# Splitting the weight slabs of the recurrent mixers one block ahead, and keeping their two parts in DRAM

## The chip, the cores and the metric

The kernel runs on one core of a Trainium2 chip. The metric is the device time of one execution in microseconds. The kernel before took 2590.76 us, the median of 3 runs (2590.26 to 2594.12). All engine times below come from one profiled execution of it.

## What is computed

Everything is fp32, on 512 tokens of width 1024. Block 1 has two layers, each with a latent attention, a dilated attention, gates, and an output projection that is added to x. Block 2 has two layers too: a mixer, then a convolutional feed-forward part. The mixer of its first layer is the recurrent one: an HGRN2 part and an RWKV7 part, side by side. Cut to what matters here:

```python
# block 1, each of 2 layers
h = rms_norm(x, norm_g[layer]); p = h @ w_in[layer]
...
x = x + jnp.concatenate([a, b], axis=-1) @ w_out[layer]
# block 2, first layer: the recurrent mixers
h = _rmsnorm(x, norm_g[l, 0]) * (1.0 + scale) + shift
p = h @ ab_w_in[j]
pa, pb = p[..., :A_IN], p[..., A_IN:]
q, f_fwd, f_bwd, i, g = jnp.split(pa, 5, axis=-1)
y_a = _hgrn2_mixer(q, f_fwd, f_bwd, i, g, lower_bounds[l], hgrn_norm_g[j])
y_b = _rwkv7_mixer(pb, rwkv_mu[j], ...)
mix = jnp.concatenate([y_a, y_b], axis=-1) @ ab_w_out[j]
x = x + gate * mix
...
x = x + gate * _conv_ffn(h, ffn_w_up[l], ffn_conv_w[l], ffn_conv_b[l], ffn_w_down[l])
```

## The kernel before

Activations lie transposed, features on the 128 partitions and the 512 tokens along the row. A product with fp32 precision is made of three TensorE passes over split operands: an operand a is held as a high part (a rounded to fp32r by ScalarE, `ACT`) and a low part (a minus the high part, by VectorE, `DVE`), and `mm3` adds high x high, high x low and low x high. A weight matrix is cut into slabs of 128 partitions x 1024 elements (512 KB): eight tiles of 128 x 128, one for each 128 rows of the contraction.

`wslab` (L70) brings one slab in: a DMA issued by the sync engine (`SP`) into a buffer `wraw`, a copy on ACT into `whi` (L75), a subtraction on DVE into `wlo` (L76). Each of the three tags has three buffers that are taken in turn, whoever asks. `gemm` (L91) takes such a slab and issues 24 matmuls of 128x512 into one PSUM tile. The three slabs that follow a norm are split early by `prepare` (L119) and multiplied by `early`.

The stages, in order:
- Block 1, twice (`block1_mixers`, L416): six gemms for the latent attention, four gates (`gate`, L426), the latent attention, V products of the dilated attention (weights `w_dv`, with the ada slabs of block 2 streamed beside them by `adaln`), then four head pairs with six gemms each (`operands`, L578) between the steps of `attention` (L604), four more gates, and `out_proj` (L191) with eight gemms on `w_out`. While it runs, x comes back from DRAM in one transfer of 2 MB (`load_x`, L1618), `add_x` (L229) adds each product to it, and it is written to DRAM again piece by piece (`to_dram`, L1608).
- The recurrent mixers (`m2`, L1680): `rwkv_lora` takes the three prepared slabs; `rwkv_g` takes three slabs for each of four head pairs P; `rwkv_p`, `rwkv_a`, `rwkv_t`, `rwkv_c1`, `rwkv_c2`, `rwkv_c3` are the recurrence, a long chain of small matmuls and vector steps. Between its steps `hgrn_fill` (L1237) computes the HGRN projections (4 slabs `w_hi`, 16 slabs `w_hg`) and writes them to DRAM (`spill`). Then the HGRN units run beside the first half of the output projection (`out_proj_steps`, eight half slabs of 128x512), and the second half (eight half slabs) follows.
- The feed-forward part, the second mixer (`m3`) and its feed-forward part.

The program is written as one stream; a scheduler places each engine's instructions in a fixed order, and each engine, and each DMA queue, works through its own in that order. SP issues nearly all DMAs, so a DMA whose buffer isn't free holds back those behind it. The buffers are taken in the order of the code:

```python
        self.w = es.enter_context(tc.tile_pool(name="w", bufs=3))
...
        hi, lo = out or [self.w.tile(shape, F32R, name=t, tag=t) for t in ("whi", "wlo")]
        nc.scalar.activation(hi, raw, AF.Copy)
        (eng or nc.vector).tensor_tensor(lo, raw, hi.bitcast(F32), op=ALU.subtract)
```

Of the kernel before, what the change touches and what calls it, by code (L numbers as in the profile page):

```python
# [24 lines left out]
class Ctx:  # L25
# [44 lines left out]
    def wslab(self, src, shape, raw=None, eng=None, out=None):  # L70
        nc = self.nc
        if raw is None:
            raw = self.wraw(src, shape)
        hi, lo = out or [self.w.tile(shape, F32R, name=t, tag=t) for t in ("whi", "wlo")]
        nc.scalar.activation(hi, raw, AF.Copy)  # L75
        (eng or nc.vector).tensor_tensor(lo, raw, hi.bitcast(F32), op=ALU.subtract)  # L76
        return hi, lo
# [41 lines left out]
    def prepare(self, src, raw=None, eng=None):  # L119
        pool, tag = ((self.px, "px"), (self.py, "py"), (self.pg, "pg"))[len(self.ready)]  # L120
        self.ready.append((self.wslab(src, [128, KD, 128], raw, eng), pool.tile([128, S], F32, name="pe", tag=tag)))

    def split(self, hi, lo, src):
# [67 lines left out]
    def out_proj_steps(self, pool, W, k0, mix, xcol, gate=None, done=None, norm=None, parts=None):  # L191
# [10 lines left out]
        for o in range(KD - late):  # L202
            xc = xcol(o)
            ps = self.gemm(W[:, o, k0:k0 + n], mh, ml, n)
            self.add_x(xc, ps, gate, o)
            if done is not None:
                done(o, xc)
            if norm is not None:
                norm.tile(o)
            yield  # L210
        if norm is not None and not late:
            norm.finish()
        if late:
            last = range(KD - late, KD)
            ws = [self.wslab(W[:, o, k0:k0 + n], [128, n, 128]) for o in last]
            ps = [pp.tile([128, S], F32, name="pl", tag=tag) for pp, tag in ((self.pg, "pg"), (self.pg, "pg"), (self.px, "px"))[:late]]
# [17 lines left out]
def at(x, k):  # L234

    return x[k] if isinstance(x, list) else x[:, k, :]


# [177 lines left out]
def block1_mixers(c, l, nm, mixf, side, w0, fill):  # L416
# [4 lines left out]
    if True:  # L421
# [114 lines left out]
        with ExitStack() as e2:  # L536
# [42 lines left out]
            def operands(p):  # L579
# [5 lines left out]
                for gi in range(3):  # L585
                    for j in range(2):
                        ps = c.gemm(I["w_dqk"][l][:, 6 * p + 2 * gi + j], hh, hl)
                        sh = c.t2("shf")
# [104 lines left out]
            for p in range(4):  # L693
# [4 lines left out]
                attention(p)  # L698
        gate(*[k for k in range(8) if k not in GT[0] + GT[1] + GT[2]])

# [101 lines left out]
def rwkv_lora(c, rp, pp, R, hh, hl):  # L802
    nc, W = c.nc, c.ins["w_rw"]
    for ct, n in enumerate(("th", "ad", "gd")):
        ps = c.gemm(W[:, ct], hh, hl)
        o = c.t2("rlo") if n == "th" else R["gd"] if n == "gd" else rp.tile([128, S], F32, name=n)
# [13 lines left out]
def rwkv_g(c, rp, pp, R, P, hh, hl):  # L820

    out = []
    for j, n in enumerate("rkv"):
        ct = 3 + 3 * P + j
        ps = c.gemm(c.ins["w_rw"][:, ct], hh, hl)
        o = rp.tile([128, S], F32, name=n, tag=n, bufs=2)
        rwkv_mix(c, pp, R, ps, ct, o)
        out.append(o)
    R[P] = {"rkv": out}
# [403 lines left out]
def hgrn_fill(c, hh, hl, spill):  # L1233

    nc = c.nc
    for h in range(4):
        if h % 2 == 0:  # L1237
            s = h // 2
            wv = [c.wslab(c.ins["w_hi"][:, s, 4 * hf:4 * hf + 4], [128, 4, 256]) for hf in range(2)]
            for i in range(4):  # L1240
# [9 lines left out]
        for z in (1, 2, 0, 3):  # L1250
            ps = c.gemm(c.ins["w_hg"][:, 4 * h + z], hh, hl)
            t = c.tmp.tile([128, S], F32, name="sp", tag="rb", bufs=2)
# [338 lines left out]
def build(tc, I, out):  # L1591
    nc = tc.nc
    with ExitStack() as es:
# [58 lines left out]

        ap = c.pool(ea, "ada", B)


# [21 lines left out]
        ea.close()  # L1677


        def m2(hh, hl, em, side, spec):  # L1680
# [9 lines left out]
            nonlocal xd  # L1690
            W, gate = I["ab_w_out"], c.mod[0, 0][:, 2, :]
            H = hgrn_setup(c)
# [180 lines left out]
XE = lambda nc: nc.vector  # L1873
CT = 8
VS = (0, 2, 2, 2, 2, 2, 2, 2, 2, 3, 2, 2)
GT = ((0, 1, 2, 3), (), ())
# [165 lines left out]
```

## Time and profile before

| what | value |
|---|---|
| median of 3 runs | 2590.76 us (2590.26 to 2594.12) |
| the profiled execution | 2591.42 us |
| its span, first to last instruction | 2589.6 us |
| granted TensorE clock, mean | 0.977 |
| busy: PE, DVE, ACT, POOL | 2495.2, 1685.8, 1063.7, 219.6 us |
| moved by DMA | 265.09 MB, mean 102 GB/s |

PE is TensorE's matmuls, PEld its weight loads, DVE VectorE, ACT ScalarE, POOL GpSimd, SP the sync engine that issues the DMAs. The ends of matmuls are modelled and overlap: a 128x512 matmul stands with about 400 ns in the table of groups, but starts follow each other faster, so a gemm's length is read from the distance between two gemms. The span runs from 0 to 2589.6 us; the first layer of block 1 ends near 542 us, the second near 1071 us, the recurrent mixers near 1625 us.

### The profile page before, as it was taken

What the parts mean: (1) busy time and instruction counts of PE and PEld (TensorE: products, weight loads), DVE (VectorE), ACT (ScalarE), POOL (GpSimd) and SP (SyncE); (2) the same over time, 40 slices, a digit from 0 to 9 for tenths busy, and PEclk for the clock granted to TensorE, in tenths of its full rate; (3) what the DMA queues carried; (4) which work ended last, traced back from release to release, by engine and by line L of the source; (5) the groups of instructions that cost most, each with busy time, mean ns of one, the idle gap of its engine ahead of it and who ended that gap; (6) DMA issues with size and microseconds to landing.
All of it is one profiled execution on the core that took longest, in us unless ns stands there. A gap on an engine that the chain in (4) does not pass through costs nothing.

```text
span 2589.6 us, 38979 instructions
## 1 busy us (share of the span) xinstructions
PE 2495.2 (96%) x15237; PEld 1999.1 (77%) x15237; DVE 1685.8 (65%) x3362; ACT 1063.7 (41%) x1899; POOL 219.6 (8%) x311
## 2 busy tenths in 40 slices
PE   8999999999999999999999988999999989999998
PEld 6769777787697777867777767878888767888887
DVE  5767666547677666586687686786454896543544
ACT  5653333526534335553434563532333424432331
POOL 0000111000001110201001140200000210100000
PEclk9999999999999999999999989999999989999999
DMA  4136211331372213321211332686324403223322
GB/s 147 46 127 238 61 58 54 106 108 39 102 267 58 58 57 104 110 61 56 81 49 50 117 107 86 203 263 202 100 85 127 143 1 101 77 86 105 94 83 80
DMA packets 91875, 265.09 MB, mean 102 GB/s; under 512 B 14372, under 2 KB 26924, under 8 KB 90796
## 3 DMA queue, kind: packets, MB, share of 16 engines
q1 hardware_dynamic: 91692, 262.61, 32.4%
q8 instruction: 120, 1.97, 0.3%
q14 instruction: 63, 0.52, 0.1%
HBM read 246.06 MB, written 16.52 MB: 101 GB/s over the span
## 4 chain that ended last, share of the span: by engine, by line
PE 82%; DVE 9%; ACT 2%; issue 2%; DMA 2%; POOL 2%; SPq 0%; ACTq 0%; DVEq 0%; POOLq 0%
PE pg L130 18%; PE pg L131 18%; PE pg L132 18%; DMA adaw<-in_ada_w_dram 2%; PE pgv L130 2%; PE pgv L132 2%; PE pgv L131 2%; PE po L683 1%; PE po L532 1%; DVE wlo L76 1%; PE tp L527 1%; PE sc L623 1%; PE po L688 1%; POOL hl L344 1%; PE phs L1362 1%
## 5 line engine op out<-in xcount | busy, mean ns | idle before, releaser
L75 ACT ACTIVATE whi<-wraw 128x1024 fp32r<-128x1024 f32 (+3 forms) x370 | 348.1, 942 | 749.2 <-PE pg L131 561.0
L130 PE MATMUL pg<-hh,whi 128*128 128x512 f32 x1560 | 630.4, 404 | 10.1 <-ACT whi L124 6.6
L131 PE MATMUL pg<-hl,whi 128*128 128x512 f32 x1560 | 628.9, 403 | 0.8 <-DVE hl L362 0.8
L132 PE MATMUL pg<-hh,wlo 128*128 128x512 f32 x1560 | 627.4, 402 | 0.5 <-DVE wlo L76 0.5
L76 DVE TENSOR_TENSOR wlo<-wraw,whi 128x1024 fp32r<-128x1024 f32 (+4 forms) x366 | 421.5, 1153 | 271.3 <-ACT whi L75 264.9
L130 PEld LDWEIGHTS pg<-hh,whi 128*128 128x128 f32 x1560 | 295.1, 189 | 87.0 <-ACT whi L124 6.6
L131 PEld LDWEIGHTS pg<-hl,whi 128*128 128x128 f32 x1560 | 295.6, 189 | 78.5 <-issue 7.5
L132 PEld LDWEIGHTS pg<-hh,wlo 128*128 128x128 f32 x1560 | 295.3, 189 | 74.9 <-issue 4.5
L130 PE MATMUL pg<-hidh,whi 128*128 128x512 f32 (+1 forms) x396 | 148.0, 374 | 0.0
L132 PE MATMUL pg<-hidh,wlo 128*128 128x512 f32 (+1 forms) x396 | 146.3, 369 | 0.0
L131 PE MATMUL pg<-hidl,whi 128*128 128x512 f32 (+1 forms) x396 | 145.6, 368 | 0.0
L719 DVE CUSTOM_DVE_ANT_0 adaw<-adaw,sc 128x1024 f32<-128x1024 f32 x96 | 116.3, 1225 | 42.5 <-DMA adaw<-in_ada_w_dram 35.3
L591 POOL TENSOR_TENSOR shf<-shf,roped 128x512 f32<-128x512 f32 x48 | 61.8, 1288 | 534.3 <-ACT whi L75 251.4
L131 PE MATMUL pgv<-wlo,hh 128*128 128x512 f32 (+1 forms) x240 | 91.0, 379 | 0.0
L130 PE MATMUL pgv<-whi,hh 128*128 128x512 f32 (+1 forms) x240 | 90.4, 376 | 0.0
L132 PE MATMUL pgv<-whi,hl 128*128 128x512 f32 (+1 forms) x240 | 89.9, 375 | 0.0
L632 ACT ACTIVATE pp<-pp,nm 128x256 f32<-128x256 f32 x128 | 63.5, 497 | 54.6 <-DVE nm L629 54.6
L132 PEld LDWEIGHTS pg<-hidh,wlo 128*128 128x128 f32 x396 | 74.4, 188 | 14.9
L131 PEld LDWEIGHTS pg<-hidl,whi 128*128 128x128 f32 x396 | 74.3, 188 | 14.0
L130 PEld LDWEIGHTS pg<-hidh,whi 128*128 128x128 f32 x396 | 74.4, 188 | 13.4
L1532 ACT ACTIVATE fu<-fu 128x512 f32<-128x512 f32 x44 | 27.8, 631 | 116.2 <-DVE fu L745 116.2
L231 DVE SCALAR_TENSOR_TENSOR xT<-pg,mod,xT 128x512 f32<-128x512 f32 (+1 forms) x54 | 38.4, 710 | 50.5 <-PE pg L132 50.4
(526 smaller groups left out, 4522.1 us busy)
## 6 DMA issues: line engine op xcount, KB each, us to landing
adaw<-in_ada_w_dram SPq DMA_DIRECT2D x96, 512.0 KB, 4.7
wraw<-in_ffn_up_dram SPq DMA_DIRECT2D x88, 512.0 KB, 3.6
wraw<-in_w_dqk_dram SPq DMA_DIRECT2D x48, 512.0 KB, 3.5
wraw<-in_ffn_down_dram SPq DMA_DIRECT2D x32, 512.0 KB, 3.6
wraw<-in_w_dv_dram SPq DMA_DIRECT2D x24, 512.0 KB, 3.7
wraw<-in_w_gate_dram SPq DMA_DIRECT2D x16, 512.0 KB, 3.7
wraw<-in_w_out_dram SPq DMA_DIRECT2D x16, 512.0 KB, 3.7
wraw<-in_w_hg_dram SPq DMA_DIRECT2D x16, 512.0 KB, 3.7
```

What stands on the lines that cost most here:

```text
L75: nc.scalar.activation(hi, raw, AF.Copy)
L76: (eng or nc.vector).tensor_tensor(lo, raw, hi.bitcast(F32), op=ALU.subtract)
L130: mm(out, lhsT=ah, rhs=bh, start=first, stop=False)
L131: mm(out, lhsT=ah, rhs=bl, start=False, stop=False)
L132: mm(out, lhsT=al, rhs=bh, start=False, stop=last)
L231: self.nc.vector.scalar_tensor_tensor(x, in0=ps, scalar=gate[:, o:o + 1], in1=x, op0=ALU.mult, op1=ALU.add)
L344: nc.gpsimd.tensor_tensor(self.hl[:, k, t], u, h, op=ALU.subtract)
L527: nc.tensor.transpose(tp[:, kt, :], pe[:, kt * 128:(kt + 1) * 128], c.ident)
L591: nc.gpsimd.tensor_tensor(sh, sh, roped[:, 1, :], op=ALU.mult)
L632: nc.scalar.activation(pz, pz, AF.Exp, bias=nm[:, z, i:i + 1], scale=0.125, accum_out=st[:, 1, z, i:i + 1])
L719: nc.vector.tensor_tensor_reduce(w, in0=w, in1=sc, scale=1.0, scalar=0.0, op0=ALU.mult, op1=ALU.add, accum_out=mod[:, j:j + 1])
L1532: nc.scalar.activation(u, u, AF.Silu)
```

## The change

A new generator, `presplit`, does the split of a slab ahead of time: it loads the raw slab, splits it on ACT and DVE into the same rotating `whi` and `wlo` buffers, and writes both parts to a DRAM tile of their own. `ahead` runs it for one more slab. Forty slabs go through it: 12 of `w_rw`, 16 of `w_hg`, 4 of `w_hi` and 8 of `ab_w_out`, in that order. It is called in block 1 only: at two of the six gemms of each head pair, at each of the last four gates, and at each gemm of the output projection except the last two of layer 1 (38 slabs: 20 in layer 0, 18 in layer 1); `c.ahead(99)` does the last two right before `m2`. In `m2`, `wslab` then issues two DMAs, one into `whi` and one into `wlo`, with no split. The output projection of `m2` reads half of a slab's columns each time, so each of its 8 slabs is read in two halves. The three prepared slabs of `rwkv_lora` are loaded and split as before.

```diff
@@ wslab @@
+        if isinstance(src, Parts):
+            hl = [self.w.tile(shape, F32R, name=t, tag=t) for t in ("whi", "wlo")]
+            for t, z in zip(hl, src.parts):
+                nc.sync.dma_start(t.bitcast(F32), z)
+            return hl
@@ new in Ctx @@
+    def presplit(self, parts):
+        for p in parts:
+            hl = self.wslab(p.src, [128, 1024])
+            p.full = []
+            for t, n in zip(hl, "hl"):
+                self.uid += 1
+                z = self.dram.tile([128, 1024], F32, name=f"ps{n}{self.uid}")
+                self.nc.sync.dma_start(z, t.bitcast(F32))
+                p.full.append(z)
+            yield
+
+    def ahead(self, n=1):
+        for _ in range(n):
+            next(self.pre, None)
@@ out_proj_steps @@
+            self.ahead(OP)
-            ps = self.gemm(W[:, o, k0:k0 + n], mh, ml, n)
+            ps = self.gemm(W[o].cut(k0, k0 + n, 128) if isinstance(W, list) else W[:, o, k0:k0 + n], mh, ml, n)
...
-            ws = [self.wslab(W[:, o, k0:k0 + n], [128, n, 128]) for o in last]
+            ws = [self.wslab(W[o].cut(k0, k0 + n, 128) if isinstance(W, list) else W[:, o, k0:k0 + n], [128, n, 128]) for o in last]
@@ new @@
+class Parts:
+    def __init__(self, src):
+        self.src = src.rearrange("p k n -> p (k n)")
+
+    def cut(self, k0, k1, n):
+        v = Parts.__new__(Parts)
+        v.parts = [z.rearrange("p (k n) -> p k n", n=n)[:, k0:k1] for z in self.full]
+        return v
@@ operands @@
+                        if j and gi < 2:
+                            c.ahead()
                         ps = c.gemm(I["w_dqk"][l][:, 6 * p + 2 * gi + j], hh, hl)
@@ the last gates of block1_mixers @@
-        gate(*[k for k in range(8) if k not in GT[0] + GT[1] + GT[2]])
+        for k in range(8):
+            if k not in GT[0] + GT[1] + GT[2]:
+                c.ahead()
+                gate(k)
@@ rwkv_g; hgrn_fill alike; rwkv_lora's becomes c.gemm(None, hh, hl) @@
-        ps = c.gemm(c.ins["w_rw"][:, ct], hh, hl)
+        ps = c.gemm(c.parts["rw"][ct - 3].cut(0, KD, 128), hh, hl)
@@ build @@
+        c.parts = {"rw": [Parts(I["w_rw"][:, k]) for k in range(3, 15)], "hg": [Parts(I["w_hg"][:, k]) for k in range(16)],
+                   "hi": [Parts(I["w_hi"][:, s, 4 * hf:4 * hf + 4]) for s in range(2) for hf in range(2)],
+                   "out": [Parts(I["ab_w_out"][:, o]) for o in range(KD)]}
+        c.pre = c.presplit([p for n in ("rw", "hg", "hi", "out") for p in c.parts[n]])
...
         ea.close()
+        c.ahead(99)
...
-            W, gate = I["ab_w_out"], c.mod[0, 0][:, 2, :]
+            W, gate = c.parts["out"], c.mod[0, 0][:, 2, :]
...
+OP = 1
```

The change also moves instructions in each engine's fixed order. In the lists below `psh` and `psl` are the DRAM tiles of the high and low parts; L136 writes them, L75 of the changed kernel reads them. Line numbers of the changed kernel are higher: L1662 is L1623 of before, L1647 is L1608, L1845 is L1800, L769 is L730, and PE's L118, L121 and L151 to L153 are L113, L116 and L130 to L132.

The first place is SP's list from the gates of layer 0 to its output projection. Before:

```order
L67 DMA wraw<-in_w_gate_dram 128x1024 x4
L67 DMA wraw<-in_w_out_dram 128x1024 x4
L1623 DMA xT<-in_x_dram 128x4096
L67 DMA wraw<-in_w_out_dram 128x1024 x2
L1608 DMA xd<-xT 128x512
L67 DMA wraw<-in_w_out_dram 128x1024
```

The load of x stood behind four slabs of `w_out`, and nothing but loads stood near it. The same place in the changed kernel, SP again, where `psh_4202` is the slab split ahead of the second gemm of the projection:

```order
L67 DMA wraw<-in_w_out_dram 128x1024
L67 DMA wraw<-in_w_hg_dram 128x1024
L136 DMA psh_4202<-whi 128x1024
L136 DMA psl_4204<-wlo 128x1024
L1662 DMA xT<-in_x_dram 128x4096
L67 DMA wraw<-in_w_out_dram 128x1024
L136 DMA psh_4249<-whi 128x1024
L67 DMA wraw<-in_w_hg_dram 128x1024
L136 DMA psl_4251<-wlo 128x1024
L67 DMA wraw<-in_w_out_dram 128x1024
L136 DMA psh_4296<-whi 128x1024
L136 DMA psl_4298<-wlo 128x1024
```

Two slabs of `w_out` now stand ahead of the load of x, and the two writes of a split slab stand right before it. A little later in SP's list of the changed kernel, around the sixth slab of `w_out`:

```order
L67 DMA wraw<-in_w_out_dram 128x1024
L67 DMA wraw<-in_w_hg_dram 128x1024
L1647 DMA xd<-xT 128x512
L136 DMA psh_4343<-whi 128x1024
L136 DMA psl_4345<-wlo 128x1024
L136 DMA psh_4390<-whi 128x1024
L136 DMA psl_4392<-wlo 128x1024
L67 DMA wraw<-in_w_out_dram 128x1024
```

The sixth slab's load stands behind four writes in a row; layer 1 has the same rows with other numbers.

The second place is the start of the recurrent mixers. SP before, where `rwkv_g`'s and `rwkv_p`'s first loads stand:

```order
L844 DMA rwkv_a_9083<-in_rwkv_a_dram 128x128
L730 DMA g_17700<-in_norm_g_dram 128x8
L67 DMA wraw<-in_w_rw_dram 128x1024 x6
L844 DMA rwkv_a_9707<-in_rwkv_a_dram 128x128
L840 DMA rw_9705<-in_rwkv_w_dram 65x2x128
```

SP in the changed kernel; `psh_9121` and `psh_9131` are the last two of the forty slabs, `psh_2034` the first slab that `rwkv_g` reads:

```order
L769 DMA g_18004<-in_norm_g_dram 128x8
L136 DMA psh_9121<-whi 128x1024
L136 DMA psl_9123<-wlo 128x1024
L136 DMA psh_9131<-whi 128x1024
L136 DMA psl_9133<-wlo 128x1024
L75 DMA whi<-psh_2034 128x1024
L75 DMA wlo<-psl_2036 128x1024
L75 DMA whi<-psh_2124 128x1024
L75 DMA wlo<-psl_2126 128x1024
```

The first slab's loads stand behind four writes. PE's list there in the changed kernel, from the end of the third prepared slab (L121, tile `pe`) on:

```order
L118 MATMUL pe<-hh,wlo 128x256
L121 MATMUL pe<-hl,whi 128x256 x16
L151 MATMUL pg<-hh,whi 128x512
L152 MATMUL pg<-hl,whi 128x512
L153 MATMUL pg<-hh,wlo 128x512
```

As before, PE has nothing between the last prepared slab and the first gemm of `rwkv_g`, and the first small matmul of the recurrence stands behind three gemms.

The third place is the end of the mixers, SP's list around the load of x for the second half of the projection. Before:

```order
L67 DMA wraw<-in_ab_w_out_dram 128x512
L1800 DMA xn<-xo 128x512 x2
L67 DMA wraw<-in_ab_w_out_dram 128x512 x2
L1623 DMA xT<-xn 128x4096
L67 DMA wraw<-in_ab_w_out_dram 128x512 x2
L67 DMA wraw<-in_ffn_up_dram 128x1024 x4
```

SP in the changed kernel:

```order
L75 DMA whi<-psh_8585 128x512
L75 DMA wlo<-psl_8587 128x512
L1845 DMA xn<-xo 128x512
L75 DMA whi<-psh_8633 128x512
L75 DMA wlo<-psl_8635 128x512
L1845 DMA xn<-xo 128x512
L1662 DMA xT<-xn 128x4096
L75 DMA whi<-psh_8681 128x512
L75 DMA wlo<-psl_8683 128x512
L75 DMA whi<-psh_8729 128x512
L75 DMA wlo<-psl_8731 128x512
L75 DMA whi<-psh_8777 128x512
```

Before, six of the eight half slabs of the second half stood ahead of this load; now three pairs do, and five pairs stand behind it.

## Rows read from the trace of the kernel before

**Rows 1.** Page, part 1: busy time of the engines, share of the span.

```profile
PE 2495.2 (96%) x15237; PEld 1999.1 (77%) x15237; DVE 1685.8 (65%) x3362; ACT 1063.7 (41%) x1899; POOL 219.6 (8%) x311
```

**Rows 2.** Busy time by stretch, us: PE, PEld, DVE, ACT, POOL, granted clock, DMA share, GB/s.

```profile
260.00:500.00 240.00, 237.92 (x1235) 184.35 (x1234) 161.61 (x438) 103.11 (x246) 26.37 (x21) 0.99 0.21 62
500.00:540.00 40.00, 40.00 (x173) 32.16 (x172) 22.32 (x28) 16.19 (x23) 0.00 (x0) 1.00 0.47 150
...
sum 535.00, PE 491.70 PEld 389.70 DVE 399.10 ACT 242.95 POOL 74.97; mean PE 163.90 PEld 129.90 DVE 133.03 ACT 80.98 POOL 24.99
```

**Rows 3.** Chain that ended last, 1095 to 1625 us: lines' shares, then start, us, what.

```profile
by line: PE pg L130 8.2%; PE pg L131 8.2%; PE pg L132 7.8%; issue 4.7%; PE phs L1362 4.0%; DVE wlo L76 3.0%; PE psh L1110 2.9%; PE psg L1099 2.2%; PE psz L1124 2.1%; PE psx L946 1.8%; PE psx L949 1.6%; PE psk L1139 1.5%; DVE hlf L764 1.4%; 
...
1120.08 0.95 ACT whi L75
1121.05 1.22 DVE wlo L76
...
1547.47 0.59 DVE wlo L76
```

**Rows 4.** Lines L76 and L75, 1090 to 1625 us: count, ns least/median/most.

```profile
L76 DVE TENSOR_TENSOR wlo<-wraw,whi x50: 676/1216/1767, 1090.4 to 1618.1; 128x1024 fp32r<-128x1024 f32 x34, 128x512 fp32r<-128x512 f32 x16
...
L75 ACT ACTIVATE whi<-wraw x51: 612/1051/1069, 1089.1 to 1618.5; 128x1024 fp32r<-128x1024 f32 x35, 128x512 fp32r<-128x512 f32 x16
```

**Rows 5.** Layer 0, 425 to 590 us: lines L429 (gates), L229 (`add_x`), first and last start.

```profile
L429 DVE TENSOR_TENSOR sg<-pg,rbx x4: 683/692/692, 463.6 to 494.4; 128x512 f32<-128x512 f32 x4
...
L229 DVE TENSOR_TENSOR xT<-xT,pg x8: 686/687/687, 500.0 to 539.2; 128x512 f32<-128x512 f32 x8
```

**Rows 6.** DMA issues, 440 to 600 us: count, KB each, us from issue to landing.

```profile
wraw<-in_w_out_dram SPq DMA_DIRECT2D x8, 512.0 KB, 3.8
xT<-in_x_dram SPq DMA_DIRECT2D x1, 2048.0 KB, 7.9
xd<-xT SPq DMA_DIRECT2D x8, 256.0 KB, 2.0
```

**Rows 7.** Stretches with DMA share near 1 (columns as in rows 2).

```profile
185.00:190.00 5.00, 5.00 (x23) 4.15 (x22) 2.46 (x3) 2.60 (x5) 0.00 (x0) 1.00 0.96 320
220.00:225.00 5.00, 5.00 (x22) 5.00 (x22) 4.03 (x7) 1.06 (x1) 0.00 (x0) 1.00 1.02 413
```

**Rows 8.** Layer 0, order of time on SP: start, us, issue.

```profile
445.22 33.36 SPq L67 DMA_DIRECT2D wraw<-in_w_out_dram  x4
486.45 0.33 SPq L1623 DMA_DIRECT2D xT<-in_x_dram  x1
496.26 2.10 SPq L67 DMA_DIRECT2D wraw<-in_w_out_dram  x2
```

**Rows 9.** Start of the mixers: pieces of the chain, start, us, what.

```profile
1091.29 1.88 PE pe L116 x16
1109.98 0.86 PE pkk L851 x2
```

**Rows 10.** Around the second half of the mixers' projection, 5 us stretches (columns as in rows 2).

```profile
1590.00:1595.00 5.00, 1.09 (x4) 0.71 (x4) 3.08 (x12) 0.27 (x1) 0.00 (x0) 0.54 0.01 3
1595.00:1600.00 5.00, 4.59 (x10) 3.16 (x11) 3.06 (x5) 2.77 (x5) 0.00 (x0) 0.50 0.00 0
```

**Rows 11.** The same place: PE in order of time at half clock and after.

```profile
1599.78 0.63 PE L130 MATMUL pg<-mhl,whi 128*128 128x512 f32 x1
1600.20 0.60 PE L131 MATMUL pg<-mhl,whi 128*128 128x512 f32 x1
...
1602.73 0.39 PE L132 MATMUL pg<-mhl,wlo 128*128 128x512 f32 x1
1602.96 0.39 PE L130 MATMUL pg<-mhl,whi 128*128 128x512 f32 x1
```

**Rows 12.** The same place: line L231, `add_x` of the second half.

```profile
L231 DVE SCALAR_TENSOR_TENSOR xT<-pg,mod,xT x5: 750/750/751, 1597.5 to 1608.0; 128x512 f32<-128x512 f32 x5
```

More of the change, by code (lines that the diff above doesn't have):

```diff
@@ L802, in rwkv_lora @@
 def rwkv_lora(c, rp, pp, R, hh, hl):
-    nc, W = c.nc, c.ins["w_rw"]
+    nc = c.nc
     for ct, n in enumerate(("th", "ad", "gd")):
-        ps = c.gemm(W[:, ct], hh, hl)
+        ps = c.gemm(None, hh, hl)
         o = c.t2("rlo") if n == "th" else R["gd"] if n == "gd" else rp.tile([128, S], F32, name=n)
@@ L1238, in hgrn_fill @@
             s = h // 2
-            wv = [c.wslab(c.ins["w_hi"][:, s, 4 * hf:4 * hf + 4], [128, 4, 256]) for hf in range(2)]
+            wv = [c.wslab(c.parts["hi"][2 * s + hf].cut(0, 4, 256), [128, 4, 256]) for hf in range(2)]
             for i in range(4):
@@ L1250, in hgrn_fill @@
         for z in (1, 2, 0, 3):
-            ps = c.gemm(c.ins["w_hg"][:, 4 * h + z], hh, hl)
+            ps = c.gemm(c.parts["hg"][4 * h + z].cut(0, KD, 128), hh, hl)
             t = c.tmp.tile([128, S], F32, name="sp", tag="rb", bufs=2)
```

## The prediction

> **What bounds the kernel now.** I read the page first, then stretches, then the chain inside the one stretch that the change relieves, and last the DMA rows of the stretches that it burdens. The page says that PE is busy for 96% of the span, and DVE and ACT are not near that [rows 1]. So a split that is taken off DVE saves time only where PE waits for it. The stretch table says where that can be: in the 535 us of the recurrent mixers PE is busy for 491.7 us [rows 2], which leaves 43.3 us idle. That is the most that this stretch could give if all its idle time went; a shorter chain can't give more while PE has the same matmuls. In the 240 us of the head pairs of layer 0, where twelve of the splits go, PE is idle for 2.1 us: anything that makes PE wait there is a loss [rows 2]. The output projection of layer 0, 500 to 540 us, shows PE without a gap and the DMA engines at a share of 0.47 [rows 2].
>
> The chain of waits then says how much of the mixers' splitting lies on the path. Between 1095 and 1625 us the line that makes `wlo` has 3.0% of 530 us, 15.9 us [rows 3]; two of its pieces, 2.4 us, are the feed-forward part's, so 13.5 us in 15 pieces are the mixers', and 3.6 us in 5 pieces are ACT's `whi` (ACT's first, and DVE's first and last, stand in [rows 3]). All splits of the stretch are 50 at a median of 1.216 us on DVE and 51 at 1.051 us on ACT [rows 4], some 55 and 49 us. So the change removes about 100 us of engine work there, and 17.1 us of chain.
>
> **The price of a transfer.** In the output projection a slab of 512 KB lands 3.8 us after its issue and the 2 MB of x 7.9 us after [rows 6]: three times 512 KB more take 4.1 us, 1.4 us each. In the densest stretches the engines move 320 to 413 GB/s [rows 7], so 512 KB take 1.64 to 1.27 us. I take 1.5 us for each 512 KB and 2.3 us that do not depend on size.
>
> **Head pairs and gates, both layers: +1 us.** Twelve slabs a layer are loaded, split (2.3 us of ACT and DVE) and written. Over 240 us this adds 15 us to DVE's 161.6 and 13 to ACT's 103.1, and three transfers of 512 KB each, 54 us of DMA work, to a share of 0.21 [rows 2]. The cover is there: a gemm takes 5.6 us (the eight `add_x` from 500.0 to 539.2 us are 5.6 apart [rows 5]), and a slab is on hand two gemms before. But a third of the 24 splits could still hold a gemm by 1.05 us: ends 0 and +8.
>
> **Output projection of layer 0: +8 us.** Its DMA work grows most. Before it was eight slabs, x, and eight pieces of 256 KB written, 8.4 MB in all; now eight slabs more come in and sixteen parts go out, 12.6 MB. That is 21 MB against some 45 us, about 470 GB/s, over the 413 that the trace shows at best [rows 7]. A part of it can lie before and behind the stretch, so I price the two places where SP's order makes a `w_out` slab late.
> - Before, SP issued four slabs by 478.6 us, x at 486.45, and the next two slabs at 496.26 [rows 8]. Now the two writes of a split slab stand right before x, and this slab's buffer comes free only when the last gate's gemm ends; that gate's DVE step starts at 494.4 [rows 5], so the gemm ends near 494.2, and the split adds 2.3: x is issued at about 496.6, ten later. The third `w_out` slab stands behind it: 2.3 + 6.0 (x) + 1.5 (itself) + 2.3 (split) lets its gemm start at 508.7, where before it followed the second at 505.0. **3.7 us late.** If x only shared the engines with it, 496.6 + 3.8 + 2.3 is 502.7: nothing. With the two writes ahead, 3.0 more: 6.7.
> - The sixth slab stands behind four writes. The last pair is split in the buffer that the fourth gemm frees, so the load is issued 2.3 us after that gemm's end, and 5.6 us later the sixth gemm should start. 2.3 + 3.8 + 2.3 is 8.4: 2.8 late with an idle queue, 5.8 if the last two writes go first, 8.8 if all four do. I take 4.3.
>
> The sum is 8.0; ends 3 and 15. **Layer 1** has the same rows and the same places: +8 again, with the same ends.
>
> The Trainium skill, "DMA: Bandwidth & Descriptors", section "Anatomy of one DMA — SWDGE (gpsimd) path", fits a transfer by about 2.0 us and its bytes over 436 GB/s, for GpSimd's queue; these transfers are SP's, and by an estimate from that page 512 KB would take 1.2 us instead of 1.5 and each layer's sum would be about 3 us smaller.
>
> **Start of the mixers: +10 us.** Before, the third prepared slab's second half runs from 1091.29 for 1.88 us, and the first pair of recurrence matmuls starts at 1109.98 [rows 9], 16.8 us later: exactly three gemms, no gap. Now the first slab of `rwkv_g` is read from DRAM into a `whi` and a `wlo` buffer. There are three of each, and the two before it in turn go to the last two of the forty slabs; this one gets the third prepared slab's, free at 1093.2, and its two reads stand behind four writes. Two reads of 512 KB land in 2.3 + 3.0 = 5.3 us alone, 8.3 with two writes before them, 11 or so with four. I take 7 (ends 5 and 11), with nothing else for PE there; as three gemms stand before the first recurrence matmul, the chain is late by as much. A gap also costs clock: around 1592 us PE was idle for about 4 us, the granted clock read 0.54 and 0.50 in the two stretches of 5 us from there on [rows 10], and starts of matmuls were 0.42 us apart where 0.23 us is usual [rows 11]. Some 6 us at half speed lose 3 us. I add 3 (ends 0 and 5).
>
> **End of the mixers: +1.5 us.** Six of eight half slabs stood ahead of the load of x, now three pairs. `add_x` of the second half runs from 1597.5, a quarter of 10.5 us apart [rows 12], 2.6 us; x takes 7.9 [rows 6], and the fourth pair, 256 KB twice, lands some 2 us behind x. Ends 0 and 4.
>
> **The mixers themselves: −14 us.** 17.1 us of chain go, less 3 us, a guess of a fifth, for what takes their place: raw slabs had three buffers of their own ahead of three split pairs; now a slab has three buffers in all, and two reads of 5.3 us may begin only when a gemm has freed one. If SP's reads stand behind a write of the HGRN results that waits, the slab is late. Ends: +5 (the new waits eat everything and more) and −43 (PE never idle).
>
> **Sum.** 1 + 8 + 8 + 10 + 1.5 − 14 = +14.5 on the profiled execution's 2591.4 us gives 2605.9; the median of the runs is 0.66 us lower, so **2605 us**. A measurement of this kernel tells about 0.2%, 5 us, from no change.
>
> **Rivals.**
> 1. *The DMA engines take it.* Transfers share the engines and x does not hold the slab behind it: 3 us for each projection, 5 for the start of the mixers, no lost clock, 1 for the head pairs, nothing at the end, −14: −2, so 2589. For it: 413 GB/s was seen [rows 7]. Against it: no stretch shows reads and writes mixed at that rate. Chance 0.17.
> 2. *Faster: DVE's queue is the bound of the mixers.* The chain has one path, but DVE works in a fixed order, and each split that it must do makes every step behind it late, on the chain or beside it. With 55 us off its 399 us and 49 off ACT's 243 [rows 2, 4], PE's idle 43 us could shrink to about 6: −37 instead of −14, in all −8.5, so 2582. It decides from −34 on: then the 28.5 us given away elsewhere are made up, and 5 more. For it: most idle time there is short and spread. Against it: PE's own pieces head the shares of the chain [rows 3], which no split touches, and with 17.1 us on the chain gone the next chain is likely little shorter. Chance 0.23.
> 3. *Worse: each new stop costs clock too.* Five stops (two in each projection, one at the start of the mixers); if the four in the projections also halve the clock, at 3 us each, +12: 2617. For it: a stop of about 4 us did that [rows 10]. Against it: two of these four stops are shorter than that. Chance 0.10.
> 4. *It does not do what it says.* 38 of the 40 slabs are split inside block 1 in the order written, and all forty are read back; only two are not hidden. That is in my sum, with no chance of its own.
>
> To the third belongs a page: the Trainium skill, "TensorE: Matmul & The Clock Gate", section "Part 1: The HAM clock gate (the "warmup" mystery)", says that the throttled clock is the default and that activity releases it. The trace agrees, with 0.54 behind the gap; by that rule every long enough stop is paid twice, and the time would be rival 3's.
>
> **How the numbers follow.** The forecast has 0.50, and its own terms keep it slower: with all low ends but the mixers' −14 it is rival 1. The range takes the forecast and most of rivals 1 and 3, and rival 2 down to 2580: **2580 to 2621**. Left out are the upper ends of both projections together (+14) and a gain of nearly all of PE's idle time. Faster by over 0.2%: 0.23; within: 0.17; slower: 0.50 + 0.10 = 0.60.
>
> **What the profile after would show.** The load of x in layer 0 issued near 496 us instead of 486, the first `add_x` near 506, the gaps of `add_x` unequal, with two above 8 us; layer 0 ending near 550; the same in layer 1. In the mixers no `wlo` in the chain, DVE near 345 us busy, PE's first gemm behind the third prepared slab after 5 to 9 us of idle time with a granted clock near a half. The stretch from that gemm on shorter by about 14 us. DMA some 84 MB more. I am wrong if the `add_x` rows keep 5.6 us with x late, if the start of the mixers has no gap, or if the mixers shorten by over 30 us or not at all.

## The result, and the profile after

The changed kernel took 2631.33 us, the median of 4 runs (2628.45 to 2634.59); the kernel before, on the same chip, 2591.17. The ratio is 1.0151, 95% interval 1.0139 to 1.0164: **slower by 40 us**. The forecast was slower, but 2605 us, and the range ended at 2621. The profiled execution took 2634.59 us, 43 more than the one of before, so the trace shows 3 us more than the medians.

The page of the change, busy time and DMA [rows 1]:

```profile
PE 2519.1 (96%) x15237; PEld 2009.8 (76%) x15237; DVE 1691.8 (64%) x3354; ACT 1067.0 (41%) x1890; POOL 222.5 (8%) x311
...
DMA packets 116069, 349.01 MB, mean 133 GB/s; under 512 B 17060, under 2 KB 29612, under 8 KB 114988
```

Its stretches of layer 0, head pairs with gates, then output projection [rows 2]:

```profile
260.00:500.00 240.00, 237.97 (x1229) 182.72 (x1228) 172.00 (x448) 115.72 (x257) 26.19 (x21) 0.99 0.41 139
500.00:545.00 45.00, 41.36 (x168) 32.14 (x167) 29.32 (x34) 19.98 (x25) 0.00 (x0) 0.96 0.91 309
```

PE's idle time is 113.7 us where it was 94.4, and its busy time is 24 us longer for the same 15237 matmuls. The second goes with the clock: the mean granted clock fell from 0.977 to 0.970, and span times what is missing to 1 gives 60 us before and 79 after. That is for the two profiled executions. In the four runs of the change it is 68 to 79 us, and in all the runs of the kernel before that stand beside the experiments 52 to 70, so the growth is uncertain: some 11 us by the middle values. In the output projection of layer 0 the DMA share went from about 0.5 to 0.91, at 309 GB/s.

To see where it grows, I set the start of the same step in both traces side by side:

| step | before | after | late by |
|---|---|---|---|
| layer 0: first gemm of the output projection | 494.2 | 494.7 | 0.5 |
| layer 0: last `add_x` [rows 5] | 539.2 | 546.4 | 7.2 |
| layer 1: second gemm | 550.5 | 560.9 | 10.4 |
| layer 1: first gemm of the output projection | 1020.4 | 1033.0 | 12.6 |
| third prepared slab ends [rows 9] | 1093.2 | 1113.1 | 19.9 |
| first gemm of `rwkv_g` | 1093.0 | 1119.1 | 26.1 |
| first `pkk` | 1109.8 | 1137.8 | 28.0 |
| first `add_x` of the second half [rows 12] | 1597.5 | 1641.3 | 43.8 |
| end of the span | 2589.6 | 2632.8 | 43.2 |

So block 1 costs 20 us, the start of the mixers 8, and **the mixers, which were to gain, cost 16**. From here on, the length of the mixers is from the first gemm of `rwkv_g` to the first `add_x` of the second half: 504.5 us before, 522.2 after. It is one reading a kernel; two kernels with the lists of before read 504.5 and 508.5, so 4 us tell nothing.

**Output projection, layer 0.** `add_x` in the change [rows 5]:

```profile
L251 DVE TENSOR_TENSOR xT<-xT,pg x8: 680/688/689, 501.6 to 546.4; 128x512 f32<-128x512 f32 x8
```

DMA issues, 440 to 600 us, KB each, us to landing [rows 6]:

```profile
wraw<-in_w_out_dram SPq DMA_DIRECT2D x8, 512.0 KB, 6.3
...
xT<-in_x_dram SPq DMA_DIRECT2D x1, 2048.0 KB, 7.9
xd<-xT SPq DMA_DIRECT2D x8, 256.0 KB, 8.3
```

SP in order of time [rows 8], and PE with its two stops (idle before, releaser):

```profile
491.15 0.33 SPq L1662 DMA_DIRECT2D xT<-in_x_dram  x1
491.57 0.38 SPq L67 DMA_DIRECT2D wraw<-in_w_out_dram  x1
...
519.16 0.32 SPq L136 DMA_DIRECT2D psh<-whi  x1
520.42 0.32 SPq L136 DMA_DIRECT2D psl<-wlo  x1
520.80 0.45 SPq L67 DMA_DIRECT2D wraw<-in_w_out_dram  x1
```

```profile
527.00 0.51 PE L151 MATMUL pg<-mh,whi 128*128 128x512 f32 x1 [3.10 <-ACT whi L80]
...
528.26 0.51 PE L153 MATMUL pg<-mh,wlo 128*128 128x512 f32 x1 [0.53 <-DVE wlo L81]
```

SP issued x at 491.15, not 496.6, and the third gemm was only 1.0 us late, counted from the first. The sixth started 3.3 us behind the end of the fifth: the load of its slab went out at 520.80, right behind the last pair of writes and 2.7 us after the fourth gemm's end. It landed 5.0 us later, and PE stood 3.1 and 0.5 us. The granted clock then reads 0.86 and 0.80 in the two stretches of 5 us from 525 on, and the distance of two `add_x` is 11.3 us there instead of 5.6. At the median a `w_out` slab took 6.3 us to land instead of 3.8, and a write of x 8.3 instead of 2.0.

**The mixers.** PE at their start, in order of time [rows 9]:

```profile
1119.13 0.79 PE L151 MATMUL pg<-hh,whi 128*128 128x512 f32 x1 [6.01 <-DMA whi<-psh]
1119.72 0.63 PE L152 MATMUL pg<-hl,whi 128*128 128x512 f32 x1
```

Busy times up to the second half of their projection (columns as in [rows 2]), and the chain of that stretch by line [rows 3]:

```profile
1119.00:1641.00 522.00, 475.11 (x5446) 372.08 (x5447) 338.06 (x783) 192.29 (x343) 75.03 (x113) 0.93 0.33 113
```

```profile
by line: PE pg L153 9.2%; PE pg L151 9.0%; PE pg L152 9.0%; issue 5.9%; PE phs L1401 3.6%; PE psg L1138 3.1%; PE psh L1149 2.9%; PE pw L918 2.3%; PE psz L1163 2.2%; DMA hproj<-spill 2.0%; PE psx L985 1.9%; PE psx L988 1.7%; PE psk L1178 1.6
```

`add_x` of the second half [rows 12]:

```profile
L253 DVE SCALAR_TENSOR_TENSOR xT<-pg,mod,xT x5: 750/751/751, 1641.3 to 1652.0; 128x512 f32<-128x512 f32 x5
```

PE waited 6.0 us for the first slab, and its first matmuls then start 0.6 to 0.7 us apart and the next ones 0.43, where 0.23 is usual; the granted clock reads 0.56 from 1119 to 1123 us. In the mixers `wlo` has left the chain and DVE has 338 us of work (377 in the same stretch of before), as forecast. But the gemms have 27% of a chain of 522 us where they had 24% of 504.5, "issue" has 5.9% where it had 4.8%, and the granted clock is 0.93 where it was 0.95.

### The profile page after: what moved, and what is told of

Its sections match the earlier page's. It is cut to its first block, busy times and chain, and to the rows that moved or that the text cites. A ratio compares the mean times of both kernels' runs of the same rounds, so it can differ in the third digit from the quotient of the medians.

```text
span 2632.8 us, 39237 instructions
## 1 busy us (share of the span) xinstructions
PE 2519.1 (96%) x15237; PEld 2009.8 (76%) x15237; DVE 1691.8 (64%) x3354; ACT 1067.0 (41%) x1890; POOL 222.5 (8%) x311
## 4 chain that ended last, share of the span: by engine, by line
PE 78%; DVE 10%; DMA 4%; issue 3%; ACT 3%; POOL 1%; SPq 0%; DVEq 0%; ACTq 0%; POOLq 0%
PE pg L153 17%; PE pg L152 17%; PE pg L151 17%; DMA adaw<-in_ada_w_dram 2%; PE pgv L151 2%; PE pgv L152 2%; PE pgv L153 2%; PE po L719 1%; PE po L566 1%; DVE wlo L81 1%; PE tp L561 1%; PE sc L659 1%; PE po L724 1%; POOL hl L378 1%; PE phs L1401 1%
## 5 line engine op out<-in xcount | busy, mean ns | idle before, releaser
L151 PE MATMUL pg<-hh,whi 128*128 128x512 f32 x1560 | 634.5, 407 | 15.9 <-ACT whi L145 6.7
L153 PE MATMUL pg<-hh,wlo 128*128 128x512 f32 x1560 | 634.7, 407 | 1.1 <-DVE wlo L81 1.0
L81 DVE TENSOR_TENSOR wlo<-wraw,whi 128x1024 fp32r<-128x1024 f32 (+2 forms) x358 | 420.6, 1177 | 268.4 <-ACT whi L80 258.7
L151 PEld LDWEIGHTS pg<-hh,whi 128*128 128x128 f32 x1560 | 297.5, 191 | 94.1 <-ACT whi L145 6.7
L153 PEld LDWEIGHTS pg<-hh,wlo 128*128 128x128 f32 x1560 | 297.7, 191 | 79.7 <-issue 5.2
L151 PE MATMUL pg<-hidh,whi 128*128 128x512 f32 (+1 forms) x396 | 147.3, 372 | 0.0
L153 PE MATMUL pg<-hidh,wlo 128*128 128x512 f32 (+1 forms) x396 | 146.0, 369 | 0.0
L153 PE MATMUL pgv<-whi,hl 128*128 128x512 f32 (+1 forms) x240 | 91.1, 379 | 0.0
L151 PE MATMUL pgv<-whi,hh 128*128 128x512 f32 (+1 forms) x240 | 90.0, 375 | 0.0
L153 PEld LDWEIGHTS pg<-hidh,wlo 128*128 128x128 f32 x396 | 74.4, 188 | 14.5
L151 PEld LDWEIGHTS pg<-hidh,whi 128*128 128x128 f32 x396 | 74.4, 188 | 14.3
L151 PE MATMUL pg<-mh,whi 128*128 128x512 f32 x164 | 66.7, 410 | 7.9 <-ACT whi L80 6.1
```

What stands on the lines that cost most here:

```text
L151: mm(out, lhsT=ah, rhs=bh, start=first, stop=False)
L153: mm(out, lhsT=al, rhs=bh, start=False, stop=last)
```

## Experiments

Two theories stood at first. "Three places": the projections, the start, and the mixers each lose by a cause of their own. "Carried over": the mixers lose only because they start late. All ratios are to the kernel before, timed on the same chip.

**Block 1 alone, mixers alone.** The first kernel keeps the writes, and the mixers read raw slabs:

```diff
-    ps = c.gemm(c.parts["rw"][ct - 3].cut(0, KD, 128), hh, hl)
+    ps = c.gemm(c.ins["w_rw"][:, ct], hh, hl)
```

> Block 1 splits and writes the forty slabs as in the change; the mixers load and split the raw slabs as before and read none of the parts. In the trace of the change PE is 19.9 us late at the end of block 1, 28 at the first gemm of rwkv_g, and 44 at the end of the mixers. Theory 'three places' (two output projections, start of the mixers, and the mixers themselves are each slower by their own cause): +20 to +23 us here, about 2612, the mixers as long as before. Rival 'carried over' (the mixers lose because they start late and at half clock, not because of what they read): the mixers lose here too, +30 to +38, about 2625.

1.0075 (1.0058 to 1.0091), +19 us; mixers 508.5. In the second kernel `ahead` does nothing, and the parts of one slab stand for all forty:

```diff
+    next(c.pre)
+    for n in c.parts:
+        for p in c.parts[n]:
+            p.full = c.parts["rw"][0].full
```

> The mixers read two parts for each slab as in the change, but block 1 is as before: one slab alone is split and written before block 1, and its parts are read for all forty, so the projections' values are not the reference's. Theory 'three places': the mixers alone cost +16 us (44 less 28), about 2607. Rival 'carried over': the mixers alone gain what the prediction took off the chain, -5 to -14, about 2580.

1.0014 (1.0002 to 1.0025), +4 us; mixers 516.1. Neither theory holds as put: the mixers alone lose little in time, but they don't gain. The two parts add up to 23 us, not 40.

**The projections: place, queue, bytes.**

```diff
-    if j and gi < 2:
+    if j:
...
+    c.ahead()
     ps = c.gemm(I["w_gate"][l][:, k], hh, hl)
...
-OP = 1
+OP = 0
```

> All forty slabs are split at the head pairs (all three places of each, 24) and at the gates (16); none in the output projections, none right before the mixers. Theory 'three places': the output projections are back at 5.6 us for each gemm, and the first gemm of rwkv_g no longer stands behind writes: 12 to 16 us of block 1's 20 and 6 of the 8 come back, about 2611. Rival 'block 1 has no room anywhere' (PE is busy for 99% there, so a split costs the same wherever it stands): about 2630 as the change.

1.0049 (1.0032 to 1.0066), +13 us: 27 of the 40 come back.

```diff
-    self.nc.sync.dma_start(z, t.bitcast(F32))
+    self.nc.gpsimd.dma_start(z, t.bitcast(F32))
```

> The change with the writes of the parts issued by GpSimd in place of SP, so that no load stands behind a write in SP's queue; the bytes are the same. If the order in SP's queue makes the projections and the first gemm late: -10 to -15 us, about 2618. If it is the bytes (21 MB in 45 us): within 3 us of the change, 2629 to 2634.

1.0223 (1.0196 to 1.025), +58 us. Both expectations missed: the writes on another queue make it worse. PE then waits 7.1 us for `add_x` in layer 0, and block 1 ends 10 us later than with the change. The trace shows one way to it, in DVE's order of time:

```profile
511.02 1.23 DVE L81 TENSOR_TENSOR wlo<-wraw,whi 128x1024 fp32r<-128x1024 f32 x1 [5.04 <-DMA psl<-wlo]
512.17 0.68 DVE L251 TENSOR_TENSOR xT<-xT,pg 128x512 f32<-128x512 f32 x1
```

The split waits for a `wlo` buffer that a write has not yet read out. The writes of GpSimd took 6.2 to 6.5 us to land where SP's took 2.9 to 3.0, and `add_x` stands behind the split in DVE's list. Freeing SP's queue of the writes was no cure, then, but this kernel also held the buffers longer, so it does not test the queue alone.

```diff
-    z = self.dram.tile([128, 1024], F32, name=f"ps{n}{self.uid}")
-    self.nc.sync.dma_start(z, t.bitcast(F32))
```

> As the run with block 1 alone, but the parts are not written: the slabs are loaded and split in block 1, and the mixers work on raw slabs. It leaves 4.2 MB of 12.6 MB of new transfers in a layer's output projection, and all of the splits. If the bytes make the output projections late: 12 us or more of the 20 come back, about 2600. If it is the splits on ACT and DVE or the raw loads in SP's queue: about 2612 as with the writes.

1.0036 (1.0022 to 1.0049), +9 us, and block 1 ends 2.0 us late instead of 23.4. The stretch of the projection of layer 0 in four kernels: block 1 alone, without writes, moved, before (columns as in [rows 2]):

```profile
500.00:545.00 45.00, 40.07 (x162) 30.62 (x161) 29.04 (x35) 20.04 (x25) 0.00 (x0) 0.96 0.88 298
```

```profile
500.00:545.00 45.00, 45.00 (x205) 36.48 (x203) 31.92 (x38) 23.72 (x30) 0.00 (x0) 1.00 0.77 237
```

```profile
500.00:545.00 45.00, 45.00 (x197) 36.17 (x197) 26.34 (x33) 17.57 (x24) 0.00 (x0) 1.00 0.47 145
```

```profile
500.00:545.00 45.00, 45.00 (x204) 36.46 (x203) 24.81 (x31) 17.41 (x24) 0.00 (x0) 1.00 0.49 156
```

With loads and splits but no writes PE has no gap. So the writes make the projection late, not the raw loads and not ACT's and DVE's work. Whether they do it by their bytes, by their place in SP's queue or by the buffers that they hold, no run separates.

**Why don't the mixers gain?** In what follows block 1 is as before, except in the two versions with the slabs moved. First a split that costs nothing: one read, both operands the same tile, six buffers.

```diff
-    hl = [self.w.tile(shape, F32R, name=t, tag=t) for t in ("whi", "wlo")]
-    for t, z in zip(hl, src.parts):
-        nc.sync.dma_start(t.bitcast(F32), z)
-    return hl
+    self.nth = (self.nth + 1) % 2
+    tag = ("whi", "wlo")[self.nth]
+    t = self.w.tile(shape, F32R, name=tag, tag=tag)
+    nc.sync.dma_start(t.bitcast(F32), src.parts[0])
+    return t, t
```

> As the run with the mixers alone, but each slab of the mixers is read once, into one buffer (six in turn), and stands for both parts: a split that costs nothing, neither ACT, DVE nor a second transfer; the projections' values are not the reference's. Theory 'supply' (two reads for each slab and three pairs of buffers make the mixers longer): PE's idle time in the mixers falls from 45 us to 30 or less and the time to about 2580. Theory 'PE is full' (the splits on the chain stood where PE had other matmuls to do, so that taking them away only brings the wait for PE forward): as long as with two reads, 2590 to 2600.

1.0006 (0.9997 to 1.0016); mixers 515.6. Even a free split gains nothing here, so neither the second read nor the three pairs of buffers is the reason. Its mixers are 11 us longer than before; from their end, `add_x` of the second half, the rest of the program takes 987.0 us instead of 992.1, which gives some of it back. More buffers with two reads:

```diff
+    tag = ("whi", "wlo", "wraw")[self.nth]
```

> As the run with the mixers alone, with the parts in nine buffers in turn (those of the raw slabs too) in place of three pairs. Theory 'supply': 5 to 10 us faster than three pairs, 2587 to 2592. Theory 'PE is full': 2594 to 2600.

1.0039 (1.0022 to 1.0055), no gain. Then a part of the slabs; the others are raw (`c.ins`, as in the first kernel):

> As the run with the mixers alone, but only the output projection's sixteen half slabs are read in two parts; the other 32 slabs are loaded and split as before. If the loss lies where the recurrence and the gemms mix: no loss here, 2588 to 2593. If it lies at the end of the mixers: 2595 to 2600.

1.0006 (0.9994 to 1.0018); mixers 508.1.

> As the run with the mixers alone, but only the twenty slabs of the HGRN projections, which fill PE between the steps of the recurrence, are read in two parts. If the loss lies in this filling: about 2597, most of the loss of the mixers alone. If each slab has its share: about half, 2593 to 2595.

1.0029 (1.0019 to 1.004); mixers 517.9. The slabs of the filling gemms alone bring the whole loss; the twelve of `w_rw` were not tried alone. And the other way round, splits made dearer:

```diff
+    if self.twice:
+        nc.vector.tensor_tensor(lo, raw, hi.bitcast(F32), op=ALU.subtract)
```

> The kernel before, with the subtraction that makes wlo done twice for the 32 slabs and the first eight half slabs of the mixers: some 44 us more on DVE, nothing else. If the splits lie on the path that sets the end (the prediction's 13.5 us of DVE on the chain): +13 us or more, 2605. Theory 'PE is full' (PE has other matmuls there): +5 or less, 2593 to 2598.

1.0054 (1.0042 to 1.0067), +14 us. By its bounds "PE is full" falls and DVE's time there is worth something; but the lists differ here too (48 of ACT's and 118 of DVE's instructions in the mixers stand elsewhere), so this alone does not show it. Taking it away and adding it both lose, which points at what changes each time: the order in which the scheduler places the instructions. Of PE's 3422 matmuls of the mixers, 602 stand elsewhere in the change (all but the longest part that kept its order), of ACT's 323 instructions 56, of DVE's 799 164, splits not counted; with block 1 alone none does. A first try at the order by hand:

```diff
-NFS = ((1, 1, 2, 2, 1), (1, 0, 0, 2, 1), ...
+NFS = ((1, 1, 2, 1, 2), (1, 0, 0, 1, 2), ...
```

> As the run with the mixers alone, but for the second and third head pair one of the HGRN projections' gemms is written behind rwkv_p in place of before it, so that PE may have a gemm to do while rwkv_p's matmuls wait for ACT. Theory 'order' (the mixers as changed lose by stops in PE's own fixed list, at rwkv_p above all, and by the clock behind them): PE's idle time falls by 3 us or more and the time by 4 to 8 us against the mixers alone. Theory 'supply': no change, within 2 us.

1.0029 (1.0017 to 1.004): a miss, but this again changes the lists. So the next kernels hold PE's list itself:

```diff
+def in_order(tc, mm):
+    row = [mm[a + k] for a, n in PE_ORDER for k in range(n)]
+    for p, q in zip(row, row[1:]):
+        tc.add_manual_dep(q, p.name, mybir.DependencyInfo(mybir.DependencyClass.NoSync, mybir.DependencyReason.DATA), reason="order")
```

> As the run with the mixers alone (two parts read for each slab, no splits), but PE's 3422 matmuls of the mixers are held in the order that they have in the kernel before; the change had moved 602 of them. Theory 'order' (the mixers as changed lose because the scheduler places PE's matmuls otherwise): the mixers are back at 525 to 529 us, 2588 to 2592 us. Rival 'reads' (the parts come late whatever the order): about 2597 as without it. If the prediction's gain is there once the order is kept: 2577 to 2583.

1.0024 (1.0015 to 1.0034); mixers 513.2.

> As the run with a free split (one read for each slab, no ACT or DVE work on it), with PE's matmuls held in the order of the kernel before. It gives the most that a split ahead of time could give to the mixers in that order. The prediction's 17 us of chain: about 2576. Theory 'PE is full': 2585 to 2591.

1.0016 (1.0007 to 1.0026); mixers 516.2. In the first of the two ACT's and DVE's lists still differ, by 28 and 98 instructions. Both are misses for PE's order as the cause. So is the version with the slabs moved and PE's order held: 1.0042 (1.003 to 1.0055), +11 us where +13 stood without; 2600 was expected if PE's order is the cause and 2609 if not, and 2602 with this interval does not decide.

> The kernel before, with all its splits, but PE's matmuls of the mixers held in the order that they have in the changed kernel. Theory 'order': the order alone costs 5 to 15 us, 2596 to 2606, with no slab read twice. Rival 'reads': within 3 us of before.

1.0124 (1.011 to 1.0138), +32 us; mixers 538.5. Holding the order of one engine can cost 32 us; but PE's old order did not bring the time back. The waits of PE in the last of these kernels (us in total, times, longest) name ACT first:

```profile
PE pw L879 <- ACT ra L873: 9.2, 4, 3.0
PE pty L1222 <- DVE Y L1218: 7.8, 4, 4.3
PE pst L1040 <- DVE rsc L1029: 6.6, 3, 4.4
```

One such place, `rwkv_p` of the third head pair, in the timeline of before, of the change, and of the free split in the old lists (below):

```profile
1282.92 1.06 ACT L75 ACTIVATE whi<-wraw 128x1024 fp32r<-128x1024 f32 x1 [4.31 <-PE pg L131]
...
1287.01 1.28 ACT L873 ACT_TABLE_LOAD   x1
...
1288.30 0.69 ACT L873 ACTIVATE ra<-pa,l_rwkv_a 128x512 f32<-128x512 f32 x1
...
1289.05 1.13 PE L879 MATMUL pw<-th,rw 65*128 65x512 f32 x2 [0.20 <-ACT ra L873]
...
1290.31 0.63 ACT L856 ACTIVATE kry<-kry 128x512 f32<-128x512 f32 x1
```

```profile
1316.63 1.28 ACT L895 ACT_TABLE_LOAD   x1
...
1317.92 0.63 ACT L895 ACTIVATE kry<-kry 128x512 f32<-128x512 f32 x1
1318.57 1.28 ACT L912 ACT_TABLE_LOAD   x1
...
1319.87 1.27 ACT L912 ACTIVATE ra<-pa,l_rwkv_a 128x512 f32<-128x512 f32 x2
...
1320.61 3.78 PE L918 MATMUL pw<-th,rw 65*128 65x512 f32 x4 [2.70 <-ACT ra L912]
```

```profile
1281.17 1.28 ACT L914 ACT_TABLE_LOAD   x1
...
1282.47 0.69 ACT L914 ACTIVATE ra<-pa,l_rwkv_a 128x512 f32<-128x512 f32 x1
...
1283.21 1.12 PE L920 MATMUL pw<-th,rw 65*128 65x512 f32 x2 [0.82 <-ACT ra L914]
...
1284.47 0.63 ACT L897 ACTIVATE kry<-kry 128x512 f32<-128x512 f32 x1
```

Before, ACT did the first `ra` ahead of the second `kry`, and `pw` waited 0.2 us. In the change, with the `whi` copy gone from ACT's list, the second `kry` and its table load of 1.28 us stand first; `pw` waits 2.7 us, and its four matmuls take 3.8 us. The stop costs clock too: the granted clock reads 0.56 from 1320 to 1324 us, where before reads 1.00 from 1289 to 1294. Over the four head pairs PE waits 8.4 us for `ra` in the change and 3.0 before, so this place is a part of the loss and not all of it. The last kernels hold the lists of PE, ACT and DVE in the mixers, all but the splits (`ORDER` has one row for each engine):

```diff
+    for name, runs in ORDER.items():
...
+        for p, q in zip(row, row[1:]):
+            c.tc.add_manual_dep(q, p.name, ...)
```

> As the run with a free split (one read for each slab, no split), but ACT's 323 and DVE's 799 instructions of the mixers that are left are held in the order of the kernel before too, not PE's 3422 alone. Theory 'order of all engines' (with PE's order kept, ACT's list was still another one, and rwkv_p's pw waited 2.8 us for ACT's ra in place of 0.2 us): the stops go and the mixers become shorter than before by what the splits held on the chain, 10 to 17 us, 2574 to 2581. Theory 'PE is full': 2586 to 2592.

**0.9933 (0.9918 to 0.9947), −17 us** (−15 by the two medians, −12.8 by the spans of the two traces); mixers 496.1. Of the 12.8 us 8.4 lie in the mixers. Another 5.1 come behind them, in the norm ahead of the feed-forward part and its first matmuls, where no list is held: from `add_x` on the program takes 987.0 us, as with the free split in the scheduler's lists.

> As the run with the mixers alone (two parts read for each slab), with the order of PE, ACT and DVE of the kernel before. Theory 'order of all engines': within 4 us of the run with the free split in that order, so 2574 to 2585; if the reads come late by themselves, 8 us or more above it.

0.9977 (0.9966 to 0.9988), −6 us; mixers 497.0. What the two reads cost is 11 us by the ratios, 9 by the medians, 5.8 by the two spans (2576.8 and 2582.6) and 0.9 in the mixers up to `add_x`; the other 5 of the spans are the stretch behind, 992.0 us here. As this kernel does no more splits in the mixers than the last one, those 5 us are not what the splits cost.

> The forty slabs split at the head pairs and gates, none in the output projections, with the order of PE, ACT and DVE of the kernel before in the mixers; the best version so far. Theory 'order of all engines': block 1's 9 us stay and the mixers give 10 to 14, so 2586 to 2592, no better than before. Theory 'PE is full': 2600.

0.9988 (0.9976 to 0.9999); mixers 498.0. This is the best whole version of the change: 3 us under before, less than the 0.2% that can be told from no change. `add_x` of the second half starts at 1589.8, 1590.5 and 1596.3 us in these three:

```profile
L255 DVE SCALAR_TENSOR_TENSOR xT<-pg,mod,xT x5: 744/751/751, 1589.8 to 1599.5; 128x512 f32<-128x512 f32 x5
```

```profile
L253 DVE SCALAR_TENSOR_TENSOR xT<-pg,mod,xT x5: 750/751/751, 1590.5 to 1600.5; 128x512 f32<-128x512 f32 x5
```

```profile
L254 DVE SCALAR_TENSOR_TENSOR xT<-pg,mod,xT x5: 750/751/753, 1596.3 to 1607.1; 128x512 f32<-128x512 f32 x5
```

## Why the prediction was right on the sign and wrong on the size

- **Head pairs and gates, +1 us:** 0.5 us in layer 0 and 2.2 in layer 1. Right within its ends.
- **Output projections, +8 each:** +9.9 and +7.3. The size was near, but one of the two places was wrong, so that is partly luck. "x is issued at about 496.6" failed: x went out at 491.15, and the third gemm was 1.0 us late where 3.7 were forecast (before, it started at 505.4 and not at 505.0). The sixth slab came as forecast, behind four writes: its gemm started 3.3 us late (4.3 forecast). But its `add_x` came 5.7 us late in all, because a second stop of 0.5 us and a lower granted clock followed, which the sum had left out. Another 3.2 us come in layer 0 right behind the projection, a place that I had not priced: PE is idle for 1.3 us there, and the granted clock reads 0.75 and 0.57 in the two stretches of 5 us from 550 on, where before shows one such stretch, 0.66 from 545 on. Without the writes the loss is gone; whether their order, as priced, or the density that I had only named, 21 MB in 45 us, made the sixth slab late is open. The Trainium skill's fit ("DMA: Bandwidth & Descriptors", section "Anatomy of one DMA — SWDGE (gpsimd) path"), 436 GB/s, was not reached here: 309 GB/s at a share of 0.91; by the Trainium skill's figure each layer would have been forecast 3 us lower, further from what was measured.
- **Start of the mixers, +10:** 6.2 us of wait and 1.9 of half clock, 8.1. Right.
- **The mixers themselves, −14, and their end, +1.5:** the failed step. Measured +16; "not at all" shorter was one of the prediction's own signs of being wrong. The bound (PE idle for 43 us) and the share of the chain (17.1 us) were read rightly; the step "17.1 us of chain go, less 3" took for granted that each engine would go through the rest of its list as before. The scheduler wrote new lists for PE, ACT and DVE. In these a free split is worth nothing in time, and the mixers get 11 us longer with it (515.6). In the old lists they get 8.4 us shorter with a free split and 7.5 with two reads (497.0), 6 by the ratio. So the share of the chain promised about twice what the splits give even with the lists held, and the new lists turned the gain into a loss: some 19 us lie between the two orders, both for the free split and for two reads.
- **Rival 2** (faster by DVE's queue) had the right object and the wrong reach: even in the old lists a free split took 8.4 us off the mixers, not 37. **Rival 3** (stops cost clock too), priced at 12 us, happened in part: the clock did fall behind the stop at the sixth slab, as above, and span times missing clock grew by some 11 us over the whole program. The forecast held 3 us of it, at the start of the mixers.
- **Sum:** measured in the trace, 2.7 + 9.9 + 7.3 + 8.1 + 15.8 − 0.6 behind = 43.2. All but the mixers came to 28 where the forecast had 27, in part because the terms of the projections missed both ways.

What stays open: block 1 alone and mixers alone make 23 us, the start of the mixers takes about 5 more than in either, and the change lost 40. The rest, some 12 us, is not pinned to a place. The clock is one candidate: by the middle of the runs, span times missing clock is 65 us with block 1 alone and 60 with the mixers alone, where the runs of before beside them have 64, and about 71 in the change. This was not tried apart. The change itself in the old lists was not run, only its version with the slabs moved.

## What to carry to other kernels

A share of the chain says what an operation costs in the lists as they stand. Where a scheduler writes them, taking the operation out is a new program: compare the lists of every engine in the stretch first, ACT's with its table loads too, and where many rows moved, price the move or hold the old lists. Even with the lists held, the splits gave about half of their share, by one reading a kernel. And work that is moved ahead needs room in DMA as much as in the engines: here the writes of parts into a stretch that already moved 8 MB cost more than the splits were worth.

## What was not expected of the hardware

Loads and writes mixed ran at 295 to 309 GB/s at DMA shares of 0.87 to 0.91 in the two projections, where a stretch of before had shown 413 at 1.02 [rows 7]. And writes issued by GpSimd landed in 6.2 to 6.5 us (median, 440 to 600 us) where SP's took 2.9 to 3.0. The loads beside them gained little: 5.5 us instead of 6.3 for a `w_out` slab, 5.2 instead of 5.3 for a `w_hg` slab, and 6.1 instead of 4.9 for a `w_in` slab.
